# The gate matrix of a dense expert mixer, built from one-hot tiles laid out per token

## The chip, the cores and the metric

One core of one Trainium2 chip. The metric is the device time of one execution in microseconds, the median over the runs of a kernel. The core has five engines that run side by side: TensorE (PE in the profile, with PEld for its weight loads), VectorE (DVE), ScalarE (ACT), GpSimd (POOL) and SyncE (SP); here SP issues the plain transfers and POOL the gathers.

## What is computed

Two decoder layers over 512 tokens of 1024 features, in float32: a token mixer (windowed attention in layer 0, a gated short convolution in layer 1) and, after each, an expert mixer. Of the latter, cut to what matters:

```python
q = (xt @ w_query).reshape(T, PEER_HEADS, 2, QUERY_HALF)
s = jnp.einsum('thpd,hpnd->thpn', q, sub_keys)
s_top, i_top = lax.top_k(s, PEER_TOPK)
...
g_s, sel = lax.top_k(cand, PEER_TOPK)
idx = jnp.take_along_axis(cand_idx, sel, axis=-1)
g = jax.nn.softmax(g_s, axis=-1)
...
a = jnp.einsum('td,thkd->thk', xc, jnp.take(expert_u, ic, axis=0))
w = gc * jax.nn.gelu(a, approximate=False)
y = jnp.einsum('thk,thkd->td', w, jnp.take(expert_v, ic, axis=0))
```

Each token picks 8 x 16 = 128 of 16384 experts, numbered 128 x (first index) + (second index), with a gate for each.

## The kernel before

Tokens come in four tiles of 128. Tiles 0 and 1 go through `gather`: POOL fetches the chosen rows of U and V one by one, VectorE multiplies and sums a row of U (ug, L639), TensorE adds up the rows of V (acc, L677). Tiles 2 and 3, 256 tokens, go through `dense`: all 16384 experts are computed for all of them, in 128 steps of 128 experts. A step has two halves. `ustep` loads a tile of U, splits it into two parts of lower precision (`halves`: uh on ScalarE, ul on VectorE), multiplies (psA, 24 matmuls of 256 columns) and applies gelu (dw). `vstep` multiplies dw by the step's row of the gate matrix G, splits the product (wh, wl), loads and splits a tile of V (vh, vl) and multiplies (y, 12 matmuls of 512 columns). `ustep` runs seven steps ahead.

G[j, i, t] is the gate that token t gives expert 128 i + j, or zero. `gen(i, tg)` makes it for 32 rows i and 16 tokens at a time, so 4 chunks of 32 steps x 16 groups of tokens = 64 gens per layer. The token's 128 second indices, compared with 0 to 127, make the one-hot tile oj; the first indices, compared with the chunk's 32, make a one-hot tile that is multiplied by the gates' high and low halves (oi). For each token two matmuls of oj against oi add up the chunk's 32 columns (psG). `iorep` holds 0 to 127, each 16 times, so that the compare runs with 16 tokens innermost:

```python
oj = pool.tile([P, P, TG], F16, name="oj", tag="oj", bufs=2)
nc.vector.tensor_tensor(oj, jT.unsqueeze(1).to_broadcast([P, P, TG]), iorep, op=ALU.is_equal)
...
nc.tensor.matmul(ps[:, T * IC:(T + 1) * IC], oj[:, :, T], oi[:, q, :, T], start=(q == 0), stop=(q == 1))
```

So `oj[:, :, T]` takes every 16th element. ScalarE then scales psG into four tiles of 8 rows of G (L759). Those tiles rotate through five buffers; one of them first holds `pre`, the gelu results of the first 8 steps, which run before G exists. The first chunk's 16 gens come in a row at the head of `dense`; a later chunk's may be issued from step 24 of the chunk before on, when its buffers are free, with a priority (`HPG`) that puts them ahead of other work. psG has one bank of PSUM.

Three streams (dense layers, gathers, routing) are interleaved by `merge`, and a scheduler then orders each engine's instructions by its own estimate of their times. On an engine they run in that order.

Of the kernel before, what the change touches and what calls it, by code (L numbers as in the profile page):

```python
# [8 lines left out]
F32 = mybir.dt.float32  # L9
# [27 lines left out]
HC = 8  # L37
# [9 lines left out]
GB = 5  # L47
# [8 lines left out]
PRE = 1  # L56
# [28 lines left out]
def trunk(ctx: ExitStack, tc: tile.TileContext, a: dict, out: bass.AP):  # L85
# [32 lines left out]
    io16 = cst.tile([P, TK], F16, name="io16")  # L118
# [3 lines left out]
    iorep = cst.tile([P, P, TG], F16, name="iorep")  # L122
    io = s2.tile([P, P], F32, name="io", tag="g", bufs=3)
    nc.sync.dma_start(io, a["io"])
    nc.vector.tensor_copy(io16, io[:, :TK])
    nc.vector.tensor_copy(iorep, io.unsqueeze(2).to_broadcast([P, P, TG]))
# [337 lines left out]
    def decode(r, h0, h1):  # L464
# [15 lines left out]
        for h in range(n):  # L480
# [3 lines left out]
            nc.vector.tensor_tensor(oh, abx, io16.unsqueeze(1).unsqueeze(1).to_broadcast(shp), op=ALU.is_equal)  # L484
# [15 lines left out]
    def route_end(r, t, psum):  # L500
# [16 lines left out]
        else:  # L517
            pst = psum("psi")
            nc.tensor.transpose(pst[:, 0:P], iif[:, 0], ident)
            nc.tensor.transpose(pst[:, P:2 * P], iif[:, 1], ident)  # L520
            nc.tensor.transpose(pst[:, 2 * P:3 * P], gf, ident)
            ijT = s2.tile([P, 2, P], F16, name="ijT", bufs=2)
            nc.vector.tensor_copy(ijT, pst[:, :2 * P].rearrange("p (a t) -> p a t", a=2))
            gT = s2.tile([P, P], F32, name="gT", bufs=1)
            nc.scalar.mul(gT, pst[:, 2 * P:3 * P], GSC)
            gb = s2.tile([P, 2, P], F16, name="gb", bufs=2)
            nc.vector.tensor_copy(gb[:, 0], gT)
            nc.vector.tensor_tensor(gb[:, 1], gT, gb[:, 0], op=ALU.subtract)
            r["ij"], r["gb"] = ijT, gb
# [163 lines left out]
    def dense(l, rs, pool):  # L693
# [11 lines left out]
        def ustep(i):  # L705
# [4 lines left out]
            w = (pre[:, i, :] if i < npre else  # L710
# [4 lines left out]
        def vstep(i):  # L715
            first, last = i == 0, i == NK - 1
            w = ws.pop(i)
            (nc.gpsimd if (WPU if st.get("gu") else WPV) else nc.vector).tensor_tensor(w, w, G[i // HC][:, i % HC, :], op=ALU.mult)
            f = VU if st.get("gu") else VG if i % IC >= 2 * IC - GB * HC else VB0
# [19 lines left out]
        def gen(i, tg):  # L739
            rr = rs[tg * TG // P]  # L740
            t0 = tg * TG % P
            iT = rr["ij"][:, 0, t0:t0 + TG]
            jT = rr["ij"][:, 1, t0:t0 + TG]
            oj = pool.tile([P, P, TG], F16, name="oj", tag="oj", bufs=2)
            nc.vector.tensor_tensor(oj, jT.unsqueeze(1).to_broadcast([P, P, TG]), iorep, op=ALU.is_equal)  # L745
            oi = pool.tile([P, 3, IC, TG], F16, name="oi", tag="oi", bufs=2)
            sh = [P, IC, TG]
            nc.vector.tensor_tensor(oi[:, 2], iT.unsqueeze(1).to_broadcast(sh), iorep[:, i:i + IC, :],
                                    op=ALU.is_equal)
            for q in range(2):  # L750
                nc.vector.tensor_tensor(oi[:, q], oi[:, 2],
# [242 lines left out]
```

## Time and profile before

| | us |
|---|---|
| median of 3 runs | 3081.59 |
| lowest, highest | 3077.46, 3094.03 |
| the profiled execution | 3084.04 |
| its span in the trace | 3082.2 |
| TensorE busy | 2782.4 (90%) |
| VectorE busy | 2255.1 (73%) |
| GpSimd busy | 1352.1 (44%) |
| ScalarE busy | 1178.1 (38%) |

The span runs from the first to the last instruction of the profiled execution; busy times overlap. TensorE's busy time counts matmuls from start to modelled end, so how far apart they start says more than how long each lasts. The chain of waits goes back from the last instruction to what released it, step by step.

### The profile page before, as it was taken

How to read it: one execution, taken by the hardware profiler on the slowest of the kernel's cores; microseconds unless marked ns; L12 is line 12 of the kernel's file. 1: busy time of each engine (PE TensorE's matmuls, PEld its weight loads, DVE VectorE, ACT ScalarE, POOL GpSimd, SP SyncE). 2: the span in 40 equal slices, each digit the busy share in tenths (PEclk: the TensorE clock that was granted, in tenths of full speed). 3: DMA queues.
4: the chain of work that ended last, by engine and by line, in shares of the span. 5: the costliest groups of instructions: out<-in, count | busy, mean ns of one | idle time of the engine just before them, and what ended most of it. 6: DMA issues, size and time to landing. Idle time of an engine off the chain costs nothing.

```text
span 3082.2 us, 53493 instructions
## 1 busy us (share of the span) xinstructions
PE 2782.4 (90%) x19980; PEld 2242.6 (73%) x19980; DVE 2255.1 (73%) x5363; ACT 1178.1 (38%) x2414; POOL 1352.1 (44%) x1154
## 2 busy tenths in 40 slices
PE   5964799999998999999997798999998798999998
PEld 5862367757986887778776787775787687778776
DVE  2499859887996997455459998887479999456444
ACT  4225433424333334344343334333434333334433
POOL 0157643354354444531347752345326866531331
PEclk8986899979999999999999899997999999999999
DMA  5888888879889977985999996787959988975996
GB/s 193 299 312 307 323 303 292 307 278 359 299 329 381 356 268 260 328 301 178 350 335 387 373 359 220 264 306 270 319 193 377 357 297 321 340 274 182 341 338 215
DMA packets 263205, 931.40 MB, mean 302 GB/s; under 512 B 29984, under 2 KB 38560, under 8 KB 262944
## 3 DMA queue, kind: packets, MB, share of 16 engines
q0 software_dynamic: 147456, 536.94, 48.1%
q1 hardware_dynamic: 115488, 391.03, 35.2%
q8 instruction: 158, 2.59, 0.3%
q14 instruction: 103, 0.84, 0.1%
HBM read 916.31 MB, written 11.53 MB: 301 GB/s over the span
## 4 chain that ended last, share of the span: by engine, by line
PE 72%; DVE 14%; DMA 5%; issue 4%; ACT 3%; POOL 1%; SPq 0%; DVEq 0%; ACTq 0%; POOLq 0%
PE y L736 20%; PE acc L677 9%; PE psG L756 9%; PE psA L180 8%; PE psA L181 7%; PE psA L183 7%; DVE ug L639 7%; PE psrq L568 3%; DMA ug<-in_u_dram,idx 2%; PE psbcu L404 1%; DMA vg<-in_v_dram,idxT 1%; PE psq L241 1%; DVE vl L702 1%; PE psrs L574 1%; PE psrq L180 1%
## 5 line engine op out<-in xcount | busy, mean ns | idle before, releaser
L667 POOL DMA_INDIRECT vg<-in_v_dram,idxT x512 | 550.0, 1074 | 945.7 <-PE acc L677 839.0
L636 POOL DMA_INDIRECT ug<-in_u_dram,idx x512 | 670.3, 1309 | 626.5 <-DVE act L639 269.8
L639 DVE CUSTOM_DVE_ANT_0 ug<-ug,xn 128x1024 f32<-128x1024 f32 x512 | 628.8, 1240 | 27.5 <-DMA ug<-in_u_dram,idx 26.7
L180 PE MATMUL psA<-xh,uh 128*128 128x256 f32 x2048 | 525.5, 294 | 44.7 <-ACT uh L701 26.8
L702 DVE TENSOR_TENSOR ul<-du,uh 128x1024 fp32r<-128x1024 f32 x256 | 316.4, 1236 | 264.5 <-ACT uh L701 244.9
L181 PE MATMUL psA<-xl,uh 128*128 128x256 f32 x2048 | 503.7, 284 | 0.0
L180 PEld LDWEIGHTS psA<-xh,uh 128*128 128x128 f32 x2048 | 391.9, 191 | 147.6 <-ACT wh L724 54.5
L702 DVE TENSOR_TENSOR vl<-dv,vh 128x1024 fp32r<-128x1024 f32 x256 | 319.9, 1249 | 183.5 <-ACT vh L701 169.4
L701 ACT CAST uh<-du 128x1024 fp32r<-128x1024 f32 x256 | 269.5, 1053 | 340.7 <-PE psA L181 296.4
L181 PEld LDWEIGHTS psA<-xl,uh 128*128 128x128 f32 x2048 | 391.5, 191 | 5.3 <-issue 3.0
L701 ACT CAST vh<-dv 128x1024 fp32r<-128x1024 f32 x256 | 268.8, 1051 | 240.8 <-PE y L736 198.3
L677 PE MATMUL acc<-vg,wd 128*32 128x512 f32 x2048 | 315.8, 637 | 10.4 <-DMA vg<-in_v_dram,idxT 10.0
L756 PEld LDWEIGHTS <-oj 128*128 128x128 f16 x4096 | 278.1, 159 | 63.1 <-issue 37.6
L736 PE MATMUL y<-vh,wh 128*128 128x512 f32 x1024 | 291.5, 404 | 26.6 <-ACT vh L701 26.6
L756 PE MATMUL psG<-oi,oj 128*128 128x32 f16 x4096 | 298.4, 249 | 7.6 <-ACT G L759 6.6
L183 PE MATMUL psA<-xh,ul 128*128 128x256 f32 x2048 | 292.2, 284 | 5.3 <-DVE ul L702 5.3
L736 PE MATMUL y<-vl,wh 128*128 128x512 f32 x1024 | 281.7, 397 | 11.6 <-DVE vl L702 11.6
L183 PEld LDWEIGHTS psA<-xh,ul 128*128 128x128 f32 x2048 | 264.4, 190 | 23.5 <-issue 9.2
L736 PE MATMUL y<-vh,wl 128*128 128x512 f32 x1024 | 278.7, 394 | 0.0
L759 ACT ACTIVATE G<-psG 128x128 f32<-128x128 f32 x512 | 102.5, 282 | 366.5 <-PE psG L756 346.2
L745 DVE TENSOR_TENSOR oj<-ijT,iorep 128x2048 f16<-128x2048 f16 x128 | 157.8, 1233 | 108.9 <-PE psG L756 108.6
L736 PEld LDWEIGHTS y<-vh,wh 128*128 128x128 f32 x1024 | 181.1, 192 | 71.4 <-ACT vh L701 35.1
(207 smaller groups left out, 3902.6 us busy)
## 6 DMA issues: line engine op xcount, KB each, us to landing
du<-in_uT_dram SPq DMA_DIRECT2D x256, 512.0 KB, 6.2
dv<-in_v_dram SPq DMA_DIRECT2D x256, 512.0 KB, 6.2
wpc<-in_wq_dram SPq DMA_DIRECT2D x64, 512.0 KB, 5.7
wpc<-in_w_in_dram SPq DMA_DIRECT2D x48, 512.0 KB, 6.7
wpo<-in_wo_dram SPq DMA_DIRECT2D x16, 512.0 KB, 4.5
ug<-in_u_dram,idx POOLq DMA_INDIRECT x512, 7.3
vg<-in_v_dram,idxT POOLq DMA_INDIRECT x512, 6.9
wpo<-in_w_out_dram SPq DMA_DIRECT2D x16, 512.0 KB, 7.3
```

Of the source, the lines that this page charges most:

```text
L180: nc.tensor.matmul(ps, w[0][:, k, :], x[0][:, k, ts], start=(k == 0), stop=False)
L181: nc.tensor.matmul(ps, w[0][:, k, :], x[1][:, k, ts], start=False, stop=False)
L183: nc.tensor.matmul(ps, w[1][:, k, :], x[0][:, k, ts], start=False, stop=(k == KC - 1))
L636: nc.gpsimd.indirect_dma_start(out=ug, out_offset=None, in_=a[f"u{l}"], in_offset=bass.IndirectOffsetOnAxis(ap=r["idx"][h][:, c:c + 1], ax ...
L639: nc.vector.tensor_tensor_reduce(out=ug, in0=ug, in1=xn, scale=1.0, scalar=0.0, op0=ALU.mult, op1=ALU.add, accum_out=act[:, s:s + 1])
L667: ld = nc.gpsimd.indirect_dma_start(out=vg, out_offset=None, in_=a[f"v{l}"], in_offset=bass.IndirectOffsetOnAxis(ap=idxT[:, tt:tt + 1], ax ...
L677: mm = nc.tensor.matmul(acc[c:c + 32, :], wd[:, j, r8, :], vgs[j][:, h * 512:(h + 1) * 512], start=(q == 0 and r8 == 0), stop=(q == 3 and ...
L701: nc.scalar.copy(hi, w)
L702: nc.vector.tensor_tensor(lo, w, hi, op=ALU.subtract)
L736: nc.tensor.matmul(ys[tt][h], x[:, tt * P:(tt + 1) * P], m[:, h * 512:(h + 1) * 512], start=first and k == 0, stop=last and k == len(terms ...
L745: nc.vector.tensor_tensor(oj, jT.unsqueeze(1).to_broadcast([P, P, TG]), iorep, op=ALU.is_equal)
L756: nc.tensor.matmul(ps[:, T * IC:(T + 1) * IC], oj[:, :, T], oi[:, q, :, T], start=(q == 0), stop=(q == 1))
```

## The change

The tiles get tokens outside and indices inside. ScalarE first spreads each token's second indices over 128 elements (jr) and its first indices and the two gate halves over 32 elements (igr, three parts), by copies with a broadcast source. VectorE compares jr with 0 to 127 (`io128`) into oj, compares the first part of igr in place, and multiplies the two gate parts by it in one instruction. TensorE then reads `oj[:, T, :]` and `oi[:, q, T, :]`, each contiguous. G becomes one tile of 40 rows used as a ring (row i modulo 40), in place of five buffers of 8 rows; its last 8 rows first hold what `pre` held. ScalarE's eviction is one instruction, or two where the chunk wraps around the ring. Indices and gates lie in one tile `ijg`. Line numbers fall by two to six (701 is now 696).

```diff
-    io16 = cst.tile([P, TK], F16, name="io16")
+    io128 = cst.tile([P, P], F16, name="io128")
...
-    iorep = cst.tile([P, P, TG], F16, name="iorep")
...
-    nc.vector.tensor_copy(io16, io[:, :TK])
-    nc.vector.tensor_copy(iorep, io.unsqueeze(2).to_broadcast([P, P, TG]))
+    nc.vector.tensor_copy(io128, io)
...
-            nc.tensor.transpose(pst[:, 0:P], iif[:, 0], ident)
-            nc.tensor.transpose(pst[:, P:2 * P], iif[:, 1], ident)
+            nc.tensor.transpose(pst[:, 0:P], iif[:, 1], ident)
+            nc.tensor.transpose(pst[:, P:2 * P], iif[:, 0], ident)
             nc.tensor.transpose(pst[:, 2 * P:3 * P], gf, ident)
-            ijT = s2.tile([P, 2, P], F16, name="ijT", bufs=2)
-            nc.vector.tensor_copy(ijT, pst[:, :2 * P].rearrange("p (a t) -> p a t", a=2))
+            ijg = s2.tile([P, 4, P], F16, name="ijg", bufs=2)
+            nc.vector.tensor_copy(ijg[:, 0:2], pst[:, :2 * P].rearrange("p (a t) -> p a t", a=2))
             gT = s2.tile([P, P], F32, name="gT", bufs=1)
             nc.scalar.mul(gT, pst[:, 2 * P:3 * P], GSC)
-            gb = s2.tile([P, 2, P], F16, name="gb", bufs=2)
-            nc.vector.tensor_copy(gb[:, 0], gT)
-            nc.vector.tensor_tensor(gb[:, 1], gT, gb[:, 0], op=ALU.subtract)
-            r["ij"], r["gb"] = ijT, gb
+            nc.vector.tensor_copy(ijg[:, 2], gT)
+            nc.vector.tensor_tensor(ijg[:, 3], gT, ijg[:, 2], op=ALU.subtract)
+            r["ijg"] = ijg
...
-            w = (pre[:, i, :] if i < npre else
+            w = (G[:, IC + i, :] if i < npre else
...
-            (nc.gpsimd if (WPU if st.get("gu") else WPV) else nc.vector).tensor_tensor(w, w, G[i // HC][:, i % HC, :], op=ALU.mult)
-            f = VU if st.get("gu") else VG if i % IC >= 2 * IC - GB * HC else VB0
+            (nc.gpsimd if (WPU if st.get("gu") else WPV) else nc.vector).tensor_tensor(w, w, G[:, i % GR, :], op=ALU.mult)
+            f = VU if st.get("gu") else VG if i % IC >= 2 * IC - GR else VB0
...
-            rr = rs[tg * TG // P]
+            ijg = rs[tg * TG // P]["ijg"]
             t0 = tg * TG % P
-            iT = rr["ij"][:, 0, t0:t0 + TG]
-            jT = rr["ij"][:, 1, t0:t0 + TG]
-            oj = pool.tile([P, P, TG], F16, name="oj", tag="oj", bufs=2)
-            nc.vector.tensor_tensor(oj, jT.unsqueeze(1).to_broadcast([P, P, TG]), iorep, op=ALU.is_equal)
-            oi = pool.tile([P, 3, IC, TG], F16, name="oi", tag="oi", bufs=2)
-            sh = [P, IC, TG]
-            nc.vector.tensor_tensor(oi[:, 2], iT.unsqueeze(1).to_broadcast(sh), iorep[:, i:i + IC, :],
+            jr = pool.tile([P, TG, P], F16, name="jr", tag="jr", bufs=1)
+            nc.scalar.copy(jr, ijg[:, 0, t0:t0 + TG].unsqueeze(2).to_broadcast([P, TG, P]))
+            igr = pool.tile([P, 3, TG, IC], F16, name="igr", tag="igr", bufs=1)
+            nc.scalar.copy(igr, ijg[:, 1:4, t0:t0 + TG].unsqueeze(3).to_broadcast([P, 3, TG, IC]))
+            oj = pool.tile([P, TG, P], F16, name="oj", tag="oj", bufs=2)
+            nc.vector.tensor_tensor(oj, jr, io128.unsqueeze(1).to_broadcast([P, TG, P]), op=ALU.is_equal)
+            oi = pool.tile([P, 2, TG, IC], F16, name="oi", tag="oi", bufs=2)
+            hot = igr[:, 0]
+            nc.vector.tensor_tensor(hot, hot, io128[:, i:i + IC].unsqueeze(1).to_broadcast([P, TG, IC]),
                                     op=ALU.is_equal)
-            for q in range(2):
-                nc.vector.tensor_tensor(oi[:, q], oi[:, 2],
-                                        rr["gb"][:, q:q + 1, t0:t0 + TG].to_broadcast(sh), op=ALU.mult)
+            nc.vector.tensor_tensor(oi, igr[:, 1:3], hot.unsqueeze(1).to_broadcast([P, 2, TG, IC]), op=ALU.mult)
             ps = pmm("psG")
             for T in range(TG):
                 for q in range(2):
-                    nc.tensor.matmul(ps[:, T * IC:(T + 1) * IC], oj[:, :, T], oi[:, q, :, T],
+                    nc.tensor.matmul(ps[:, T * IC:(T + 1) * IC], oj[:, T, :], oi[:, q, T, :],
                                      start=(q == 0), stop=(q == 1))
-            for hf in range(IC // HC):
-                nc.scalar.mul(G[i // HC + hf][:, :, tg * TG:(tg + 1) * TG],
-                              ps.rearrange("p (t i) -> p i t", i=IC)[:, hf * HC:(hf + 1) * HC, :], 1.0 / GSC)
+            psv = ps.rearrange("p (t i) -> p i t", i=IC)
+            r0 = i % GR
+            cut = min(IC, GR - r0)
+            for o, n, row in ((0, cut, r0), (cut, IC - cut, 0)):
+                if n:
+                    nc.scalar.mul(G[:, row:row + n, tg * TG:(tg + 1) * TG], psv[:, o:o + n, :], 1.0 / GSC)
 
         NG = T2 // TG
-        G = {}
+        G = pool.tile([P, GR, T2], F32, name="G")
 
         def gens(c, tg):
-            if tg == 0:
-                for hf in range(IC // HC):
-                    G[c * (IC // HC) + hf] = pool.tile([P, HC, T2], F32, name="G", tag="G", bufs=GB)
             with tc.high_priority(offset=HPG):
                 gen(c * IC, tg)
 
-        npre = HC * PRE
-        pre = pool.tile([P, HC, T2], F32, name="pre", tag="G", bufs=GB) if PRE else None
+        npre = GR - IC
```

The scheduler makes a new order from it. ScalarE in the late part of layer 0's dense loop, where G for the last 32 steps is made: the casts uh and vh of the weight tiles, gelu (dw), the cast wh, and G's eviction. Before, three gens to two steps:

```order
L759 ACTIVATE G<-psG 128x8x16 x4
L701 CAST uh<-du 128x1024
L712 ACTIVATE dw<-psA 128x256
L759 ACTIVATE G<-psG 128x8x16 x4
L701 CAST vh<-dv 128x1024
L724 CAST wh<-dw 128x256
L759 ACTIVATE G<-psG 128x8x16 x4
L701 CAST uh<-du 128x1024
L712 ACTIVATE dw<-psA 128x256
L701 CAST vh<-dv 128x1024
L724 CAST wh<-dw 128x256
```

And now, at the same place:

```order
L758 ACTIVATE G<-psG 128x24x16
L758 ACTIVATE G<-psG 128x8x16
L696 CAST uh<-du 128x1024
L738 COPY jr<-ijg 128x2048
L707 ACTIVATE dw<-psA 128x256
L740 COPY igr<-ijg 128x1536
L696 CAST vh<-dv 128x1024
L719 CAST wh<-dw 128x256
L758 ACTIVATE G<-psG 128x24x16
L758 ACTIVATE G<-psG 128x8x16
L738 COPY jr<-ijg 128x2048
L696 CAST uh<-du 128x1024
```

Each gen brings a jr and an igr between the casts, and four evictions of 8 rows become two, of 24 and 8.

ScalarE in the burst of gens at the head of layer 0's `dense` (abx is a spread and i a cast of the routing). Before:

```order
L759 ACTIVATE G<-psG 128x8x16 x4
L482 CAST abx<-ab 128x512
L759 ACTIVATE G<-psG 128x8x16 x8
L455 CAST i_6023<-i16u 128x32
L759 ACTIVATE G<-psG 128x8x16 x12
L482 CAST abx<-ab 128x512
L759 ACTIVATE G<-psG 128x8x16 x4
```

Now:

```order
L758 ACTIVATE G<-psG 128x32x16
L738 COPY jr<-ijg 128x2048
L740 COPY igr<-ijg 128x1536
L478 CAST abx<-ab 128x512
L758 ACTIVATE G<-psG 128x32x16
L738 COPY jr<-ijg 128x2048
L740 COPY igr<-ijg 128x1536
L478 CAST abx<-ab 128x512
L758 ACTIVATE G<-psG 128x32x16
```

Between two evictions there stand now the two spreads of a later gen; before there was routing work or nothing.

## Rows read from the trace of the kernel before

**Rows 1.** The page, part 4: shares of the chain by line.
```profile
PE y L736 20%; PE acc L677 9%; PE psG L756 9%; PE psA L180 8%; PE psA L181 7%; PE psA L183 7%; DVE ug L639 7%; PE psrq L568 3%; DMA ug<-in_u_dram,idx 2%; PE psbcu L404 1%; DMA vg<-in_v_dram,idxT 1%; PE psq L241 1%; DVE vl L702 1%; PE psrs L574 1%; PE psrq L180 1%
```
**Rows 2.** Busy time by stretch, eight stretches with gens, four shown, and their sum.
```profile
core 0: us, PE busy (x) PEld busy (x) DVE busy (x) ACT busy (x) POOL busy (x), PEclk, DMA share, GB/s
540.00:680.00 140.00, 130.17 (x1126) 92.82 (x1126) 115.84 (x426) 51.22 (x131) 65.69 (x54) 0.84 0.80 280
680.00:870.00 190.00, 183.73 (x1439) 159.06 (x1440) 160.95 (x304) 79.62 (x165) 74.82 (x64) 0.99 0.90 331
1020.00:1200.00 180.00, 169.00 (x1410) 149.83 (x1409) 161.48 (x417) 69.44 (x167) 70.38 (x61) 0.97 0.80 278
1355.00:1460.00 105.00, 105.00 (x946) 89.05 (x944) 65.80 (x100) 42.37 (x107) 11.60 (x13) 1.00 0.56 197
...
sum 1170.00, PE 1110.09 PEld 922.50 DVE 964.69 ACT 454.56 POOL 468.08; mean PE 138.76 PEld 115.31 DVE 120.59 ACT 56.82 POOL 58.51
```
**Rows 3.** The chain in time, late stretch: start us, length us, what.
```profile
1380.48 0.95 PE psA L183 x8
1381.42 2.73 PE y L736 x12
1384.16 1.00 PE acc L677 x8
1385.15 2.21 PE psG L756 x32
...
1390.96 2.17 PE psG L756 x32
...
1396.92 2.15 PE psG L756 x32
...
1400.32 2.73 PE y L736 x12
```
**Rows 4.** The chain in time, burst at the head of layer 0's dense loop.
```profile
643.82 2.24 PE psG L756 x32
646.06 1.86 PE acc L677 x8
647.92 2.26 PE psG L756 x32
```
**Rows 5.** Busy time and granted clock (PEclk) in that burst and that late stretch.
```profile
636.00:660.00 24.00, 23.81 (x216) 12.54 (x214) 17.36 (x60) 5.63 (x27) 13.03 (x13) 0.50 0.70 235
1365.00:1450.00 85.00, 85.00 (x807) 74.17 (x806) 54.98 (x83) 33.48 (x89) 9.62 (x10) 1.00 0.52 178
```
**Rows 6.** Weight loads: by source line (ns min/median/max), and a group (mean).
```profile
L756 PEld LDWEIGHTS <-oj x4096: 141/160/191, 569.0 to 2835.5; 128*128 128x128 f16 x196
...
L180 PEld LDWEIGHTS psA<-xh,uh x2048: 186/188/336, 534.6 to 3046.9; 128*128 128x128 f32 x187
...
L677 PEld LDWEIGHTS acc<-vg,wd 128*32 128x32 f32 x2048 | 51.5, 111 | 109.3 <-issue 97.4 <-POOL wd L659 0.5 <-POOL dw L718 0.4
```
**Rows 7.** ScalarE's groups (busy us, mean ns), then its timeline (start, length us).
```profile
L701 ACT CAST uh<-du 128x1024 fp32r<-128x1024 f32 x256 | 269.5, 1053 | 340.7 <-PE psA L181 296.4 <-issue 12.6 <-DVE ul L702 12.1
L482 ACT CAST abx<-ab 128x512 f16<-128x512 f32 x64 | 39.6, 618 | 39.9 <-DVE ab L478 30.7 <-DVE oh L484 5.6 <-DVE wl L725 3.4
...
1380.87 1.07 ACT L701 CAST uh<-du 128x1024 fp32r<-128x1024 f32 x1
1381.81 0.41 ACT L712 ACTIVATE dw<-psA 128x256 f32<-128x256 f32 x1
```
**Rows 8.** Groups of the gens on VectorE and ScalarE, and a float32 subtraction.
```profile
L702 DVE TENSOR_TENSOR ul<-du,uh 128x1024 fp32r<-128x1024 f32 x256 | 316.4, 1236 | 264.5 <-ACT uh L701 244.9 <-issue 16.6 <-ACT dw L712 1.5
L745 DVE TENSOR_TENSOR oj<-ijT,iorep 128x2048 f16<-128x2048 f16 x128 | 157.8, 1233 | 108.9 <-PE psG L756 108.6
L751 DVE TENSOR_TENSOR oi<-oi,gb 128x512 f16<-128x512 f16 x256 | 98.2, 425 | 1.2
L759 ACT ACTIVATE G<-psG 128x128 f32<-128x128 f32 x512 | 102.5, 282 | 366.5 <-PE psG L756 346.2 <-POOL dw L718 15.8 <-DVE pre L718 1.7
```

More of the change, by code (lines that the diff above doesn't have):

```diff
@@ L36 @@
 IC = 32
-HC = 8
 GAT = 6
@@ L46 @@
 HPT = 0
-GB = 5
+GR = 40
 WPB = 4
@@ L55 @@
 DEC = 2
-PRE = 1
 FD1 = 80.0
@@ L483, in decode @@
             oh = s2.tile(shp, F16, name="oh", bufs=1)
-            nc.vector.tensor_tensor(oh, abx, io16.unsqueeze(1).unsqueeze(1).to_broadcast(shp), op=ALU.is_equal)
+            nc.vector.tensor_tensor(oh, abx, io128[:, :TK].unsqueeze(1).unsqueeze(1).to_broadcast(shp), op=ALU.is_equal)
             nc.vector.tensor_tensor(oh, oh, r["i16"][:, h0 + h].unsqueeze(2).to_broadcast(shp), op=ALU.mult)
@@ L781, in dense @@
             c, q = divmod(i, IC)
-            q0 = 2 * IC - GB * HC
+            q0 = 2 * IC - GR
             if q >= q0 and c + 1 < NK // IC:
```

## The prediction

> **What bounds the kernel now.** I read the chain of waits first, then the busy time of the stretches in which the gate matrix G is made, then the costliest instructions, then the order in time. The chain [rows 1] is TensorE's at every large entry: the products y and psA, the gathers' acc, and psG, the small products that make G, with 9% of the span, some 270 us. G is made in 128 pieces ("gens") of 32 matmuls, 64 per layer, and the eight stretches that hold nearly all of them last 1170 us [rows 2]: TensorE is busy for 1110 us of them, VectorE for 965, ScalarE for 455. So TensorE's time in psG is nearly all on the path (128 x 2.17 = 278 us), and ScalarE has the most room.
>
> One repeating pattern shows it best [rows 3]. From y at 1381.42 to the same y at 1400.32 are 18.9 us, with two steps of the dense loop, one group of acc and three gens of 2.2 us; TensorE has no gap in it. A gen's 32 matmuls take 2.17 us, 68 ns each, though they stream only 32 columns, while the 8 of psA with 256 columns take 0.95 us, 119 ns each. 256 columns at 2.4 GHz are 107 ns, so psA has 12 ns beside its columns; 32 columns would be 13 + 12 = 25 ns. Some 40 ns in each of 4096 matmuls are not columns. In the burst of gens at the head of a layer [rows 4] a gen takes 2.24 us too, at half the clock: there [rows 5] the granted clock is 0.50 (1.2 GHz), in the late pattern 1.00 (2.4 GHz). What makes a gen long does not follow TensorE's clock.
>
> The load of weights is what the pair waits on [rows 6]. A load of 32 f32 columns lasts 111 ns on average; one of 128 f32 columns 186 at the shortest and 188 in the median, so 0.8 ns a column and 26 ns for 32. The load of oj lasts 141, 160 and 191 ns: 30 ns above the 32-column row at its shortest, and with a median far from it. In `oj[:, :, T]` one token's weights lie 16 elements apart, and so do the columns of `oi`; every other operand of the dense loop is contiguous. A clock-free, scattered cost with strided operands is how a read of memory looks that is not contiguous. That is the reading I go by.
>
> By the Trainium skill (Advanced Engine Details and Errata, Memory Cachelines), SBUF is read in 16-byte lines and an operand that touches a new line with each element pays for it. The trace agrees with the sense of it, 68 ns against the 25 just worked out, but holds no contiguous f16 weights to prove it.
>
> **The change, part by part.**
>
> *TensorE.* The same 4096 matmuls, with both operands contiguous. Below: 25 ns each, the psA row. Above: 68, if the stride is not the cause; below that row nothing excludes a gain and nothing suggests a loss, since fewer memory lines are read. I take 40: nearer to 25, because 128 columns must still be loaded for 32 streamed, and half the bytes of the f32 load (0.8 x 128 = 103 ns) would be 51. So (68 - 40) x 32 = 0.9 us a gen, 115 us in all if everything counted; the ends are 0 and 43 x 32 = 1.4 us a gen, 176 us.
>
> *ScalarE.* Two spreads are added to each gen: jr with 2048 elements, igr with 1536. The nearest rows [rows 7] are abx, the same kind of broadcast, 618 ns for 512 elements, and uh, 1053 for 1024: 0.85 ns an element. jr is then 0.618 + 1536 x 0.00085 = 1.92 us, igr 0.618 + 1024 x 0.00085 = 1.49. Bounds: below, nothing shows a cheaper element; above, abx taken whole, 618 / 512 = 1.2 ns an element, makes 2.5 and 1.9 us. I take 0.85, the step between the two rows. G's eviction was four of 128 elements at 0.28 [rows 8], 0.79 together; now it is one of 512 elements, or two that sum to that: 0.6 to 0.8, no change. Instructions queued back to back start 0.13 us before the last one's record ends [rows 7]. So a gen costs ScalarE 1.92 + 1.49 - 0.26 = 3.15 us more, 400 us in all: 455 becomes 855 of 1170 us, 73%. In the late pattern it is 3 x (1.92 + 1.49 + 0.78) + 2 x (1.05 + 1.05 + 0.41 + 0.41) = 18.4, less 20 x 0.11 for the overlap: 16.2 us, against TensorE's 18.9 - 2.7 = 16.2. There the two meet, and that caps what the shorter load can give.
>
> *VectorE.* oj's compare is 1233 ns for 2048 elements before [rows 8]: with f16 operands contiguous over 16 it is already at 0.60 ns an element, when the f32 subtractions take 1.2 ns. I give it nothing. The two multiplies of 512 (425 ns each) become one of 1024: by (1233 - 425) / 1536 = 0.53 ns an element 0.69, so 0.16 us a gen, 20 us of VectorE's time, hidden where TensorE is the bound. If VectorE were the bound, that would be a gain of 20 us.
>
> *New waits.* jr and igr have one buffer each. jr of the next gen waits for oj's compare of this one, igr for its multiply. ScalarE works in order, so behind a waiting spread stand the casts uh and vh, for which VectorE's ul and vl and then psA and y wait. In the new order of the late pattern each of these casts stands next to a spread. They have one tile in hand (two buffers of hi and lo), some 5 us; a spread of 1.9 us is covered as long as ScalarE's whole load is.
>
> *At nothing:* the ring of 40 rows in place of five blocks of 8 plus `pre` (rows come free at the same steps, 40 in each); io128 for io16 and iorep (once, at the start); the merged ijg; SP's and GpSimd's transfers, the same in number and size.
>
> *The sum by stretch*, with 0.9 us a gen:
> - Two bursts, 34 gens. 13 of each 17 come with acc alone. A gen and its acc took 2.24 + 1.86 = 4.1 us [rows 4]; now ScalarE needs 3.15 + 0.65 and some routing casts, about 4.0. That gives 13 x 0.1, and 4 gens x 0.9: 5 us a layer, 10.
> - Four middle stretches, 62 gens, as 680 to 870 and 1020 to 1200 [rows 2]: TensorE 94 to 97% busy, but VectorE 85 to 90% and the transfers' share 0.80 to 0.90, so about 70% of the saving stays: 62 x 0.9 x 0.7 = 39.
> - Two late stretches as 1355 to 1460, 30 gens: 18.9 falls to ScalarE's and TensorE's 16.2 and what an in-order queue at its limit loses, 1 us: 1.7 per three gens, 17.
>
> Together 66 us. The profiled execution took 3084.0 us, so 3018. Its time is 2.5 above the median of the runs, 3081.6; I predict **3016 us**, 2.1% faster. With 25 ns a matmul the same sum is 10 + 62 x 1.4 x 0.9 + 10 x 2.7, and a few us in the bursts: 120 at most, 2965.
>
> **The rivals.**
>
> *The load is not slow from the stride.* Loading 128 f16 columns may simply take 60 ns. For it: against the f32 rows, 103 ns for 128 columns, the 60 ns of a pair are already 1.7 times as fast, stride and all. Against it: its median lies 19 ns above its shortest, the f32 load's only 2 [rows 6]. Then psG stays at 2.2 us, the path does not shrink, and ScalarE at 16.2 of 18.9 us adds small waits, 0 to 0.3 us a gen: 3080 to 3120, by the middle 3100.
> The Trainium skill (TensorE: Matmul & The Clock Gate, Weight-path perf modes) says that fast weight load is on for 128 weights that are not fp32, packed or strided, and measures about twofold. By that rule this rival holds, and the 1.7 bears it out as far as a trace without contiguous f16 weights can.
>
> *ScalarE becomes the bound (slower).* The place is the casts uh and vh behind jr in the middle and late stretches, 92 gens. The price is one jr, 1.9 us, where a cast does not get past it in time. It decides where ScalarE's 16.2 us per three gens grow past TensorE's 16.2 to 18.9, so if a spread element costs abx's whole 1.2 ns (16.2 + 3 x 0.9 = 18.9) or the order leaves it idle for 2.7 us. If half of the 92 gens pay it, that is 87 us, less the 66 gained: 3103; if TensorE's load did not shorten either, 3150 and more. For it: the strict order and single buffers. Against it: 73% load over the stretches.
>
> *Half the gain.* Transfers or VectorE take the place of TensorE in the middle stretches, where they run at 0.80 to 0.90 [rows 2]. Then only late stretches and bursts count: about 27 us, 3055.
>
> **How the numbers follow.** Forecast 0.45, half the gain 0.13, the load unchanged 0.25, ScalarE the bound 0.17. A measurement of this kernel can tell about 0.5%, 15 us, from no change. Faster by more are the forecast and the half: 0.58. Within it lies the lower part of the unchanged load, 0.16; slower are its upper part, 0.09, and ScalarE's case: 0.26. The range from 2965 (25 ns) to 3110 takes in the forecast, the half, nearly all of the unchanged load and part of ScalarE's case. The likeliest case alone is 2965 to 3050.
>
> **What would show it.** Right: the gen's 32 matmuls in 1.3 us or so, oj's load nearer 111 ns, jr at 1.9 and igr at 1.5 us, psG's share of the chain near 5%, ScalarE busy near 1580 us, and the late pattern at 17 us. The first step is wrong if psG stays at 68 ns a matmul; the second if y and psA wait for ScalarE in the late stretches by more than 2 us per three gens. A VectorE compare well under 1.2 us would mean that I misjudged its operands.

## The result and the profile after

The changed kernel takes **2997.6 us** (median of 4 runs, 2992.0 to 3000.8) against 3083.9 us for the kernel before in the same comparison: a ratio of **0.9715**, 95% interval 0.9683 to 0.9748, 2.9% faster. The forecast was 3016 us, in a range of 2965 to 3110. The profiled execution is one of 2992.0 us, with a span of 2990.3 us, 91.9 less than before.

Part 1 of the page of the changed kernel, busy time by engine:

```profile
PE 2626.9 (88%) x19980; PEld 2083.9 (70%) x19980; DVE 2235.7 (75%) x5234; ACT 1559.1 (52%) x2384; POOL 1365.3 (46%) x1154
```

TensorE is busy for 155.5 us less (2782.4 before), ScalarE for 381 more. The gens' loads and matmuls by source line (ns min/median/max, then the first and the last start):

```profile
L751 PEld LDWEIGHTS <-oj x4096: 94/96/147, 578.0 to 2790.6; 128*128 128x128 f16 x196
L751 PE MATMUL psG<-oi,oj x4096: 175/176/251, 578.0 to 2790.6; 128*128 128x32 f16 x196
```

The load is 96 ns in the median, with 2 ns between it and the shortest, where the strided one had 160 and 19 [rows 6]. It even lies under the load of 32 f32 columns (111). The chain in time of the changed kernel, in layer 1's last gens (start us, length us, what), answers to [rows 3]:

```profile
2740.92 0.94 PE psA L179 x8
2741.87 0.81 PE psG L751 x32
2742.68 2.84 PE y L731 x12
2745.52 1.85 PE acc L672 x16
...
2748.39 0.81 PE psG L751 x32
...
2751.31 2.77 PE y L731 x12
2754.08 0.81 PE psG L751 x32
```

A gen went from 2.2 us to 0.81: 25 ns for each matmul, and the starts of two neighbours in the trace lie 25.6 ns apart on average, against 66.5 before. The rest of the pattern has the lengths it had. The largest groups that the change touches (busy us, mean ns, idle before), and what TensorE waited for longest in the dense loops and gathers (us in total, times, longest):

```profile
L738 ACT COPY jr<-ijg 128x2048 f16<-128x2048 f16 x128 | 243.2, 1900 | 35.0 <-DVE oj L742 33.1 <-DVE ijg L519 1.5
L740 ACT COPY igr<-ijg 128x1536 f16<-128x1536 f16 x128 | 188.6, 1473 | 26.9 <-DVE oi L747 24.8 <-DVE wd L655 0.6 <-DVE idxf L490 0.4
L742 DVE TENSOR_TENSOR oj<-jr,io 128x2048 f16<-128x2048 f16 x128 | 157.4, 1229 | 78.0 <-PE psG L751 66.7 <-ACT igr L740 4.8 <-ACT jr L738 3.3
L751 PE MATMUL psG<-oi,oj 128*128 128x32 f16 x4096 | 124.5, 178 | 39.8 <-DVE oi L747 30.1 <-ACT G L758 4.5 <-ACT i L451 2.8
L747 DVE TENSOR_TENSOR oi<-igr 128x1024 f16<-128x1024 f16 x128 | 90.7, 709 | 1.0
```
```profile
PE acc L672 <- DMA vg<-in_v_dram,idxT: 30.9, 28, 4.3
PE psG L751 <- DVE oi L747: 30.1, 18, 6.7
PE y L731 <- ACT vh L696: 29.9, 17, 5.3
PE psA L176 <- ACT uh L696: 19.0, 13, 1.8
```

**Where the time went.** psG's busy time on TensorE fell from 298.4 to 124.5 us, by 173.9. Other matmuls took 18.4 more, and TensorE's idle time rose from 299.8 to 363.4 us, by 63.6; 173.9 - 18.4 - 63.6 gives the 91.9 us of the span. Most of the new idle time is in two of the rows just shown: psG waits 30 us for its operand oi (0.3 before) and acc 31 us for a gathered row (10.0 before). The waits for ScalarE's casts hardly moved: y's for vh were 26.6 us before, psA's for uh 26.8.

By stretch, from the first and last y of each layer: the dense stages' y took 45.3 us less in layer 0 (1017.2 to 971.9) and 66.3 less in layer 1 (952.3 to 886.0). Up to the first y, 7.2 us were lost, and between the layers, in convolution and routing, 12.5. In that last stretch lie 472 matmuls of acc instead of 320; they take 24 us more there, and psG 23 us less, so the 12.5 us are idle time. Part of layer 1's gain is such a move: 19 us less of acc lie in its dense stage (552 matmuls instead of 704). The gathers end earlier: layer 1's last acc starts at 2796 us and not at 3046. From 2800 to 2978 us TensorE has no gap, and GpSimd does nothing.

VectorE is the bound in layer 1's middle stretch. Busy time there, and in layer 0's late stretch (columns: stretch, its length, PE, PEld, DVE, ACT, POOL, each with its instructions, PEclk, DMA share, GB/s):

```profile
1340.00:1424.00 84.00, 83.86 (x908) 62.41 (x905) 56.54 (x75) 71.88 (x91) 35.94 (x30) 1.00 0.83 293
...
2178.00:2400.00 222.00, 178.06 (x1427) 150.19 (x1425) 221.52 (x342) 131.79 (x165) 152.01 (x103) 0.92 0.95 351
```

In the first TensorE has no gap, and ScalarE is at 86%. In the second VectorE is busy throughout and TensorE for 80%: VectorE's row products ug of the gathers, 100 at 1.23 us each, take 122 of the 222 us.

### The profile page after: what moved, and what is told of

Read it like the earlier page. It is cut to its first block, busy times and chain, and to the rows that moved or that the text cites. A ratio compares the mean times of both kernels' runs of the same rounds, so it can differ in the third digit from the quotient of the medians.

```text
span 2990.3 us, 53463 instructions
## 1 busy us (share of the span) xinstructions
PE 2626.9 (88%) x19980; PEld 2083.9 (70%) x19980; DVE 2235.7 (75%) x5234; ACT 1559.1 (52%) x2384; POOL 1365.3 (46%) x1154
## 5 line engine op out<-in xcount | busy, mean ns | idle before, releaser
L662 POOL DMA_INDIRECT vg<-in_v_dram,idxT x512 | 572.2, 1118 | 689.1 <-PE acc L672 571.7
L672 PE MATMUL acc<-vg,wd 128*32 128x512 f32 x2048 | 318.1, 635 | 31.4 <-DMA vg<-in_v_dram,idxT 30.9
L731 PE MATMUL y<-vh,wh 128*128 128x512 f32 x1024 | 290.2, 406 | 34.9 <-ACT vh L696 29.9
L731 PE MATMUL y<-vh,wl 128*128 128x512 f32 x1024 | 285.5, 399 | 3.0 <-DVE wl L720 3.0
L738 ACT COPY jr<-ijg 128x2048 f16<-128x2048 f16 x128 | 243.2, 1900 | 35.0 <-DVE oj L742 33.1
L731 PEld LDWEIGHTS y<-vl,wh 128*128 128x128 f32 x1024 | 190.1, 191 | 62.9 <-DVE vl L697 18.8
L731 PEld LDWEIGHTS y<-vh,wl 128*128 128x128 f32 x1024 | 194.8, 192 | 50.9 <-DVE wl L720 4.7
L742 DVE TENSOR_TENSOR oj<-jr,io 128x2048 f16<-128x2048 f16 x128 | 157.4, 1229 | 78.0 <-PE psG L751 66.7
```

The source lines that it names most:

```text
L662: ld = nc.gpsimd.indirect_dma_start(out=vg, out_offset=None, in_=a[f"v{l}"], in_offset=bass.IndirectOffsetOnAxis(ap=idxT[:, tt:tt + 1], ax ...
L672: mm = nc.tensor.matmul(acc[c:c + 32, :], wd[:, j, r8, :], vgs[j][:, h * 512:(h + 1) * 512], start=(q == 0 and r8 == 0), stop=(q == 3 and ...
L731: nc.tensor.matmul(ys[tt][h], x[:, tt * P:(tt + 1) * P], m[:, h * 512:(h + 1) * 512], start=first and k == 0, stop=last and k == len(terms ...
L738: nc.scalar.copy(jr, ijg[:, 0, t0:t0 + TG].unsqueeze(2).to_broadcast([P, TG, P]))
L742: nc.vector.tensor_tensor(oj, jr, io128.unsqueeze(1).to_broadcast([P, TG, P]), op=ALU.is_equal)
```

## The experiments

Theory A, which the prediction rests on: the weights' contiguity gives the gain, and ScalarE's spreads are hidden. Rivals: the moving operand's contiguity gives it; the ring and its fewer evictions give it; ScalarE's load eats part of it. Each run is compared with the kernel before in the same series, so the ratios are what can be set side by side, and not the times: the changed kernel stands at 0.9715.

### One operand of TensorE strided again

The first form kept the spreads, and let VectorE write the tile in steps:

```diff
-oj = pool.tile([P, TG, P], F16, name="oj", tag="oj", bufs=2)
-nc.vector.tensor_tensor(oj, jr, io128..., op=ALU.is_equal)
+oj = pool.tile([P, P, TG], F16, name="oj", tag="oj", bufs=2)
+nc.vector.tensor_tensor(oj.rearrange("p j t -> p t j"), jr, io128..., op=ALU.is_equal)
...
-nc.tensor.matmul(ps[:, T * IC:(T + 1) * IC], oj[:, T, :], oi[:, q, T, :],
+nc.tensor.matmul(ps[:, T * IC:(T + 1) * IC], oj[:, :, T], oi[:, q, T, :],
```

That is `wts_strided`; `mov_strided` does the same to oi, `both_strided` to both.

> The changed kernel with one thing put back: the one-hot tile oj, which TensorE loads as weights, lies column by token again (32 bytes from one weight to the next), written so by VectorE; the spreads on ScalarE, the other operand and the ring stay as changed. Theory A (the contiguous weights give the gain): the psG matmuls go from 25 ns apart back to 60 to 68 ns, oj's loads from 96 ns to 140 to 190 ns, and the time to the old one plus what ScalarE's spreads cost, 3075 to 3120 us. Rival B (the moving operand's contiguity gives it): spacing stays near 25 ns, 2990 to 3015 us. Rival C (both operands add up): 45 to 55 ns, 3040 us. VectorE's write in steps may cost it up to 1 us more for each generation, which either theory allows.

> The changed kernel with the moving operand oi put back alone: one element every 32 bytes for the 32 columns of a token, written so by VectorE; weights contiguous. Theory A (weights): psG matmuls stay 25 to 32 ns apart, time 2990 to 3015 us, the same as the changed kernel within 0.5%. Rival B (moving operand): 60 to 68 ns, 3075 to 3120 us. Rival C: 40 to 50 ns, 3035 us.

> The changed kernel with both of TensorE's operands strided as before, everything else (ScalarE's spreads, the ring, the order) as changed: what is left is what the spreads and the ring cost. Theory A with dear spreads: 3100 to 3130 us, slower than the kernel before by 0.5 to 1.5%. Theory A with hidden spreads: within 0.5% of the kernel before, 3070 to 3100 us. If the ring or the spreads give part of the gain themselves: under 3065 us. The spacing of psG should be 60 to 68 ns in each case.

Measured: 3929.3 us (ratio 1.2661, 1.2608 to 1.2714), 3432.2 us (1.1048, 1.1014 to 1.1082) and 4392.7 us (1.4137, 1.4081 to 1.4193), all far outside every expectation. The groups of VectorE say why, of the first and of the second kernel:

```profile
L742 DVE TENSOR_TENSOR oj<-jr,io 128x2048 f16<-128x2048 f16 x128 | 1156.4, 9034 | 69.3 <-PE psG L751 41.2 <-ACT jr L738 16.3 <-remote 6.7
```
```profile
L747 DVE TENSOR_TENSOR oi<-igr 128x1024 f16<-128x1024 f16 x128 | 582.7, 4553 | 0.9
```

Written in steps of 32 bytes, the compare takes 9.0 us and not 1.23, the multiply 4.55 and not 0.71: some 4.4 ns an element. I had allowed 1 us a gen. As times these three runs tell nothing of TensorE, but the distance of the psG matmuls can be read from them: 62.7 ns with strided weights, 59.4 with the strided moving operand, 66.8 with both. The second was a surprise, since by Theory A it should have stayed under 32.

So both halves were made again with VectorE writing in order, from the table iorep as before, and with the spread of that operand gone from ScalarE (the other stays). First the weights, `wts_clean`, then the moving operand, `mov_clean`:

```diff
-nc.scalar.copy(jr, ijg[:, 0, ...])
-oj = pool.tile([P, TG, P], ...)
-nc.vector.tensor_tensor(oj, jr, io128..., op=ALU.is_equal)
+oj = pool.tile([P, P, TG], ...)
+nc.vector.tensor_tensor(oj, ijg[:, 0, ...].unsqueeze(1)..., iorep, op=ALU.is_equal)
```
```diff
-nc.scalar.copy(igr, ijg[:, 1:4, ...])
-oi = pool.tile([P, 2, TG, IC], ...)
+oi = pool.tile([P, 2, IC, TG], ...)
+nc.vector.tensor_tensor(hot, ijg[:, 1, ...].unsqueeze(1)..., iorep[:, i:i + IC, :], op=ALU.is_equal)
+for q in range(2):
+    nc.vector.tensor_tensor(oi[:, q], hot, ijg[:, 2 + q:3 + q, ...]..., op=ALU.mult)
```

> The changed kernel with the weights' tile oj strided again, made as before by one compare that writes in order (from the repeated index table), so VectorE's 1.23 us stays and ScalarE loses only the spread jr; the moving operand stays contiguous. The gathers of V stand early in the order, as in the changed kernel (the last one ends before 238 of the 256 expert blocks of layer 1's dense stage have been started and not at 255). If the distance of the psG matmuls is what made the gain: psG 61 ns apart and 3065 to 3100 us. If the earlier place of the gathers made half of it: 3030 to 3060 us. If either operand's stride were harmless: 2980 to 3010 us.

> The changed kernel with the moving operand oi strided again, made as before by VectorE writing in order (one compare, two multiplications), so ScalarE loses only the spread igr; the weights stay contiguous; 219 groups of acc as in the changed kernel (222). If the moving operand's stride alone holds the psG matmuls at 60 ns, as with the dear strided write: 3060 to 3105 us, ratio 0.995 to 1.007, close to the twin with strided weights (1.005). If only the weights mattered (the prediction's reason): 25 to 32 ns and 2985 to 3015 us.

Measured: `wts_clean` 3101.9 us, ratio **1.0051** (1.0034 to 1.0067); `mov_clean` 3065.5 us, **0.9944** (0.9922 to 0.9966). The second is what was expected of a stride that holds the matmuls at 60 ns; the first lies 2 us above that range. The loads of oj and psG's group, of wts_clean and then of mov_clean:

```profile
L751 PEld LDWEIGHTS <-oj x4096: 140/165/178, 570.2 to 2873.3; 128*128 128x128 f16 x196
...
L751 PE MATMUL psG<-oi,oj 128*128 128x32 f16 x4096 | 275.9, 215 | 33.8 <-DVE oi L747 33.0 <-ACT abx L480 0.7
```
```profile
L753 PEld LDWEIGHTS <-oj x4096: 95/117/128, 566.2 to 2839.8; 128*128 128x128 f16 x196
...
L753 PE MATMUL psG<-oi,oj 128*128 128x32 f16 x4096 | 269.4, 238 | 23.1 <-DVE oi L748 15.4 <-ACT G L760 4.6 <-DVE oj L742 2.6
```

psG's busy time by the layout of the two operands:

| weights | moving operand | distance, ns | psG busy, us | kernel |
|---|---|---|---|---|
| strided | strided | 66.5 | 298.4 | before |
| strided | contiguous | 62.6 | 275.9 | wts_clean |
| contiguous | strided | 59.4 | 269.4 | mov_clean |
| contiguous | contiguous | 25.6 | 124.5 | changed |

Distance here is the mean from one start to the next within a gen. Either stride alone keeps five sixths of the cost or more (one operand made contiguous saves 23 or 29 of 174 us), and the gain comes only with both. It does not come from the place of the gathers: they stand early in both kernels too (the last acc starts at 2964 and 2901 us, 3046 before). Theory A is right that a stride is the cause and wrong on which operand: 128 strided weights and 32 strided columns each take about 60 ns. That the load of one matmul runs while the columns of another stream, so that the slower of the two sets the distance, would explain it; it is argued, and the four rows are measured. The length of the load's record does not tell the distance: contiguous weights last 96 ns in the record beside a contiguous moving operand and 117 beside a strided one. Why `wts_clean` is 1.1% slower than `mov_clean`, when psG differs by only 6.5 us, is open.

The Trainium skill (TensorE: Matmul & The Clock Gate, Weight-path perf modes) says that the fast weight load is on for 128 weights that are not fp32, packed or strided. If that means the same speed in either case, the runs differ: 165 ns against 96 for the load. The 16-byte lines of the Trainium skill (Advanced Engine Details and Errata, Memory Cachelines) agree in sense with both rows of one strided operand.

### The ring alone

In the kernel before:

```diff
-G[c * (IC // HC) + hf] = pool.tile([P, HC, T2], F32, name="G", tag="G", bufs=GB)
+G = pool.tile([P, GR, T2], F32, name="G")
...
-for hf in range(IC // HC):
-    nc.scalar.mul(G[i // HC + hf][:, :, ...], ps...[:, hf * HC:(hf + 1) * HC, :], 1.0 / GSC)
+for o, n, row in ((0, cut, r0), (cut, IC - cut, 0)):
+    if n:
+        nc.scalar.mul(G[:, row:row + n, ...], psv[:, o:o + n, :], 1.0 / GSC)
```

> The kernel before with only the ring of 40 rows for G in place of five buffers of 8 rows, and the four evictions of a generation merged to one or two; operands, compares and multiplications as before. Theory A (operand layout gives the gain): same within 0.5%, 3070 to 3100 us; ScalarE's evictions give back some 0.5 us per generation where it does not end the chain. Rival D (the ring or the fewer evictions give part): 3030 to 3065 us. Psg spacing 66 ns in either.

Measured: 3154.4 us against 3107.8, ratio **1.0144** (1.0109 to 1.0178), slower, which none of the theories had. Nothing that the ring touches became dearer: psG's busy time is 297.9 us. But acc, the gathers' matmuls, is at 366.5 us:

```profile
L677 PE MATMUL acc<-vg,wd 128*32 128x512 f32 x2048 | 366.5, 639 | 5.9 <-DMA vg<-in_v_dram,idxT 4.8 <-issue 1.1
```

It was 315.8 before, with the same 2048 matmuls of the same mean length. They stand in 290 groups on TensorE instead of 238, because the scheduler put other matmuls between them. The next run shows the same.

### ScalarE's spreads made once per layer

```diff
-jr = pool.tile([P, TG, P], F16, name="jr", tag="jr", bufs=1)
-nc.scalar.copy(jr, ...)
+if "jr" not in once:
+    once["jr"] = pool.tile([P, TG, P], F16, name="jr")
+    nc.scalar.copy(once["jr"], ...)
+...
```

> The changed kernel with ScalarE's spreads made once per layer and used for all 64 generations (the gate matrix is then that of 16 tokens: this leaves the spreads of the others out). ScalarE is 3.4 us per generation lighter, psG stays contiguous at 25 ns; but in the order that results the gathers of V stand late again, as in the kernel before (the last ends with block 256). If ScalarE's load costs what the matmuls gave (rival of the prediction): 2940 to 2975 us. If the load is hidden and the gathers' place is neutral: 2980 to 3010 us. If the gathers' earlier place made part of the gain: 3020 to 3065 us, slower than the changed kernel although it does less.

The kernel leaves out the spreads of all but the first 16 tokens of a layer; the compare of the first indices writes a tile of its own here.

Measured: 3042.6 us, ratio **0.9855** (0.9839 to 0.9871), inside the third expectation: with 390 us less work on ScalarE it is slower than the changed kernel. psG is the same 124.5 us, acc is at 360.7, in 288 groups. The timeline of TensorE in this kernel (start us, length us, what) shows what a split does:

```profile
2860.74 0.62 PE L731 MATMUL y<-vh,wl 128*128 128x512 f32 x2
2861.29 1.05 PE L672 MATMUL acc<-vg,wd 128*32 128x512 f32 x2
2862.26 0.50 PE L731 MATMUL y<-vh,wl 128*128 128x512 f32 x1
2862.69 1.04 PE L672 MATMUL acc<-vg,wd 128*32 128x512 f32 x2
...
2867.96 1.07 PE L672 MATMUL acc<-vg,wd 128*32 128x512 f32 x8
2868.96 0.39 PE L177 MATMUL psA<-xl,uh 128*128 128x256 f32 x1
```

Two matmuls of acc hold TensorE from 2861.29 to 2862.26, 0.97 us; eight from 2867.96 to 2868.96, 1.00 us. They use 32 columns of the array each, and those of one group run side by side: eight of 628 ns each on average end within 1.07 us. Split in four, the same eight would cost some 3.9 us. The changed kernel has 222 groups: 66 more at 0.9 us would be 59 us, of which acc's busy time shows 42.6, and the ratios differ by 1.4%, 43 us.

In both runs the gathers also stand later in the order. To see whether that or the splitting is the cause, one number was changed in each, HPV, the priority of acc in the scheduler's order. The last gather stays at block 256, after the last of the dense loop's steps:

```diff
-HPV = 600
+HPV = 300
```

> The run with the spreads made once per layer (it leaves out the other generations' spreads), with the priority of the gathers' matmuls acc at 300 instead of 600. Their place in the order stays as late (last with block 256), but they stand in 233 groups on TensorE instead of 288 (a group of two matmuls took 1.04 us and one of eight 1.06 us, so each group more costs some 0.9 us). If the splitting is what made that run slower than the changed kernel (3042.6 against 2997.6 us): 55 groups fewer x 0.9 = 50 us, 2985 to 3005 us, ratio about 0.97. If the late place did it: 3030 to 3050 us. What then stands below the changed kernel is the price of ScalarE's spreads: nothing if they are hidden, 30 to 60 us if not.

> The kernel before with only the ring, with the priority of the gathers' matmuls at 300: late place kept (block 256), 241 groups of acc instead of 290 (the kernel before has 238). If the ring alone lost 1.4% to the splitting: 49 groups x 0.9 = 44 us back, a ratio of 0.995 to 1.005 to the kernel before. If the ring or the place itself costs it: still 1.010 to 1.018. If fewer evictions help by themselves, as between the changed kernel and its twin with the old buffers (0.9%): 0.985 to 0.995.

Measured: 3007.0 us, ratio **0.9747** (0.9728 to 0.9766), 2 us above the first expectation, and 3085.2 us, **0.9997** (0.9985 to 1.0009), inside it. Acc's groups, of the first and of the second:

```profile
L672 PE MATMUL acc<-vg,wd 128*32 128x512 f32 x2048 | 321.1, 642 | 50.6 <-DMA vg<-in_v_dram,idxT 49.1 <-ACT yg L682 1.6
```
```profile
L677 PE MATMUL acc<-vg,wd 128*32 128x512 f32 x2048 | 321.6, 643 | 9.7 <-DMA vg<-in_v_dram,idxT 9.6
```

acc is back at 321 us, and with it 1.1% in one kernel and 1.5% in the other. So the splitting was the loss in both. The ring by itself costs and gives nothing where ScalarE has room. And without nearly all its spreads the changed kernel is no faster (0.9747 against 0.9715): they are hidden. How well, within about 1%, is left open, since the two also differ in where the gathers stand: with late gathers acc waits 49 us for its rows, against 31.

### The old buffers for G in the changed kernel

```diff
-G = pool.tile([P, GR, T2], F32, name="G")
+G[c * (IC // HC) + hf] = pool.tile([P, HC, T2], F32, name="G", tag="G", bufs=GB)
...
+for hf in range(IC // HC):
+    nc.scalar.mul(G[i // HC + hf][:, :, ...], ps...[:, hf * HC:(hf + 1) * HC, :], 1.0 / GSC)
```

> The changed kernel with five buffers of 8 rows for G and four evictions per generation in place of the ring; all else as changed. If the ring is worse by itself (it cost the kernel before 1.4%): 2950 to 2985 us. If that loss came from the place of the gathers in the order, which here stays where the changed kernel has it (last at block 226 against 227): within 0.5% of the changed kernel, 2985 to 3015 us. If fewer evictions help: 3015 to 3030 us.

Measured: 3026.3 us, ratio **0.9801** (0.9785 to 0.9817), 0.9% slower than the changed kernel; the third expectation. acc is not split (316.4 us). ScalarE's evictions are 103.3 us in 512 pieces, where the changed kernel has 224 of 89.7 us, and TensorE's wait for the cast uh doubles (19.0 in the changed kernel, where the wait for oi was 30.1):

```profile
PE psA L177 <- ACT uh L697: 39.8, 25, 4.5
PE psG L752 <- DVE oi L748: 38.4, 20, 7.4
```

So merged evictions may be worth something once the spreads fill ScalarE, though nothing before. The two waits grew by 21 and 8 us, and the kernel is slower by 0.9%, some 27 us; but its order of instructions differs too, and no run parts the two causes.

### Without the spreads: VectorE reads the repeated operand itself

```diff
-nc.scalar.copy(jr, ijg[:, 0, ...])
-nc.vector.tensor_tensor(oj, jr, io128..., op=ALU.is_equal)
+nc.vector.tensor_tensor(oj, ijg[:, 0, ...].unsqueeze(2).to_broadcast([P, TG, P]), io128..., op=ALU.is_equal)
```

The compare and the multiply of the first indices likewise read ijg, without igr.

> The changed kernel without ScalarE's spreads: VectorE reads the indices and gates itself, repeated along the innermost dimension, and writes the same contiguous tiles. psG stays 25 ns apart, the gathers stand early (last at block 219). If VectorE's compare runs at the same 1.2 us from such an operand, the spreads were not needed: 2960 to 3000 us. If it takes about twice as long (2.2 us and 1.1 us more in all per generation, on the engine that is fullest in the first stretches of each layer): 3000 to 3050 us.

Measured: 3162.9 us, ratio **1.0249** (1.0232 to 1.0266), worse than the second expectation. VectorE's groups of this kernel:

```profile
L738 DVE TENSOR_TENSOR oj<-ijg,io 128x2048 f16<-128x2048 f16 x128 | 293.0, 2290 | 44.5 <-PE psG L748 44.4
L743 DVE TENSOR_TENSOR oi<-ijg,hot 128x1024 f16<-128x1024 f16 x128 | 157.4, 1230 | 0.2
L741 DVE TENSOR_TENSOR hot<-ijg,io 128x512 f16<-128x512 f16 x128 | 89.7, 701 | 0.1
```

An operand repeated along the innermost dimension makes the compare 2.29 us long and not 1.23, the multiply 1.23 and not 0.71, the small compare 0.70 and not 0.45: 1.8 us a gen more, 235 us of VectorE's time in all. That is what the spreads buy. The Trainium skill (VectorE: DVE Perf Modes, the perf-mode tier table) gives a two-input operation of 2048 bf16 elements 1224 ns in the fast mode and one of float32 2293; the trace agrees with both figures, 1229 and 2290, and so with the reading that the repeated operand puts it into the slow one. The Trainium skill (VectorE: DVE Perf Modes, Mode 1× (REGULAR)) says that odd strides work in the slow mode. Here the write in steps took 9.0 us, four times the slow mode's figure.

### The gathers earlier still

```diff
-HPV = 600
+HPV = 2000
```

> The changed kernel with the priority of the gathers' matmuls at 2000: the same 222 groups, but placed earlier still (last with block 212 of 256 against 227). If the place matters by itself: 2960 to 2985 us. If only the number of groups matters: 2985 to 3010 us, within 0.5% of the changed kernel. If earlier gathers hold up the dense stages, which then wait for VectorE and the DMA queues: 3010 to 3040 us.

Measured: 3027.7 us, ratio **0.9819** (0.9800 to 0.9838), 1% slower than the changed kernel; the third expectation. acc takes 284.3 us, the least of all runs, and TensorE is busy for 25 us less, but it waits longer for the operand oi:

```profile
PE psG L751 <- DVE oi L747: 74.0, 24, 10.7
PE psA L176 <- ACT uh L696: 55.0, 37, 4.6
```

While psG waited for oi, VectorE worked on row products of the gathers for 30.7 us, against 7.1 in the changed kernel: earlier gathers put more of them in among the gens. No run here is faster than the changed kernel.

## Why the prediction was right

**What bounds the kernel.** TensorE in psG was the right place: its busy time fell by 174 us, and the span by 92. The reason given was half of it. "The load of weights is what the pair waits on" holds in so far as strided weights alone keep the matmuls 62.6 ns apart, but the pair waits nearly as long, 59.4 ns, for the strided columns of oi, which I had named and priced at nothing by itself. Had the change made only the weights contiguous, the same reasoning would have forecast the same gain, and the run that comes nearest to that shows 0.6%. That the change took both operands was luck as far as the reasoning goes.

**TensorE's term.** I took 40 ns a matmul, between 25 and 68; it is 25.6, the lower end, from the row of psA. The step that leaned on half of the f32 load's bytes (51 ns for 128 columns) mis-sized it: the contiguous load lasts 96 ns in the record, under the f32 load of 32 columns, while the matmuls stand 25.6 ns apart, so its length is not what spaces them. The term is 1.36 us a gen and 174 in all, not 0.9 and 115. The working of the lower end, 13 ns of columns and 12 beside them, is not borne out either, though its 25 is. Some gens of the changed kernel ran at 1.2 GHz, one of them here (its start and length, then its stretch with the granted clock, 0.50):

```profile
666.27 1.03 PE L751 MATMUL psG<-oi,oj 128*128 128x32 f16 x32
...
666.20:667.10 0.90, 0.90 (x35) 0.83 (x32) 0.00 (x0) 0.00 (x0) 0.50 (x1) 0.50 0.86 328
```

Their matmuls start 27.3 ns apart, and 32 columns at that clock are 26.7 ns by themselves: 12 more would have made 39.

**What of it stays.** I kept 66 of 115 us, 57%; 92 of 174 stayed, 53%. By stretch the shares were off. The burst of layer 0, from its first gen to the first y, gave 2 us (96.1 to 94.3) where 5 were forecast: psG took 24 us less in it, but TensorE then waited 10.8 us for gathered rows and 9.0 for oi. Layer 1's burst shrank by 17 us, of which 13 are 96 matmuls of psA that now stand ahead of it. Nearly all came in the dense loops, 45 and 66 us with the move of acc, while the stretch between the layers, which I had not costed, lost 12.5. In layer 1's middle stretch the wait that comes next was named rightly (VectorE, with transfers at 0.95), as the row of 2178 to 2400 us shows.

**ScalarE.** jr at 1.900 and igr at 1.473 us were forecast at 1.92 and 1.49; busy 1559 us, forecast near 1580. The late pattern, three gens and two steps, was to stop at ScalarE's 16.2 us, and that price held. In the 84 us from 1340 to 1424 ScalarE ran 12 spreads of each kind (two gens had theirs already), the evictions of 14 gens and the casts and gelus of 10 steps, 12 x 3.37 + 14 x 0.70 + 10 x 2.92 = 79.5 us of instructions in 71.9 us of busy time, or 0.90 of it. For three gens and two steps that is 0.90 x 18.05 = 16.3 us. TensorE's part at the new lengths is 18.9 - 3 x (2.17 - 0.81) = 14.8 us, so it would have had to wait, and it did not. What the forecast had not seen is that the order would put more of acc there: 112 matmuls in those 84 us, eight to a gen, where the pattern before had eight to three gens. With them three gens took 18 us, not 17, and TensorE had no gap.

**VectorE.** oj's compare 1229 ns, forecast unchanged; the multiply 0.709, forecast 0.69. That nothing was to be gained there holds only because the spreads keep it in its fast form, as the run without them shows.

**At nothing.** The ring is worth nothing in the kernel before, as forecast, and with the old buffers the changed kernel is 0.9% slower, about 27 us: there the prediction counted 0.79 us a gen for four evictions and 0.6 to 0.8 for one or two, and called it no change. It is 103.3 / 128 = 0.81 against 89.7 / 128 = 0.70, and that small term may count where ScalarE is nearly full; no run shows it apart from the order.

**The rivals.** That the load is not slow from the stride is out: 165 against 96 ns. ScalarE did not become the bound, though it came near it in the late stretch: y's waits for vh grew from 26.6 to 29.9 us, psA's for uh fell from 26.8 to 19.0, and the run without nearly all spreads is no faster. Half the gain lay near: it named the right takers, VectorE and the transfers; psG's waits for oi and acc's for rows make 51 of the 63.6 us of new idle time. What no rival had is the order. The scheduler arranges the gathers anew with each change, and that moved the variants by 1 to 1.5%. The splitting happened not to touch this comparison: acc stands in 238 groups before and 222 after, and takes 315.8 and 318.1 us. The place of the gathers did change, and no run shows what that alone is worth in the changed kernel: the nearest one, with late gathers and without nearly all spreads, stands at 0.9747.

**The signs.** The gen's matmuls (0.81 us), jr, igr and ScalarE's busy time came as named or better. psG's share of the chain, named as near 5%, cannot be read: the chain of the changed kernel can be followed over 28% of its span only.

## What to carry to other kernels

For short 16-bit matmuls look at both operands: here a stride of 32 bytes on either side held each one near 60 ns, and only both contiguous brought 25. To get there, don't let VectorE write in steps (six to seven times the time) or read an operand repeated along the innermost dimension (1.6 to 1.9 times); let an engine with room spread it. Before a variant's time is put down to its edit, count what the scheduler did to the rest: here groups of side-by-side matmuls that were split cost as much as half the gain, and one priority undid it.

## What had not been expected of the hardware

- A compare of 2048 16-bit elements written every 32 bytes took 9.03 us, against 1.23 in order; a multiply of 1024, 4.55 against 0.71.
- The moving operand: 32 columns of 16 bits, 32 bytes apart, held a matmul at 59.4 ns, contiguous ones at 25.6, with contiguous weights in both.
- The load of 128 contiguous f16 columns took 96 ns, less than that of 32 f32 columns (111).
- Two acc matmuls of 32 array columns held TensorE for 0.97 us, eight for 1.00.
